# A decoder block in fp32r parts: gate and up of both FFNs as seven block products, in two phases

## The chip, the cores and the metric

The kernel runs on one core of a Trainium2 chip. The metric is the device time of one execution in microseconds. The engines are TensorE (PE in the profile; its weight loads are PEld), VectorE (DVE), ScalarE (ACT), GpSimd (POOL) and SyncE (SP), which only issues transfers here.

## What is computed

One layer for 1,024 tokens with 1,024 channels: an FFN, a merge of three mixers (RWKV-7, sparse attention, attention onto memory tokens), a second FFN and a last norm.

```python
def _rmsnorm(x, g):
    xf = x.astype(jnp.float32)
    y = xf * lax.rsqrt(jnp.mean(xf * xf, axis=-1, keepdims=True) + NORM_EPS)
    return (y * g.astype(jnp.float32)).astype(x.dtype)

def _swiglu(h, w_gate, w_up, w_down):          # w_gate, w_up: 1024 x 2816, w_down: 2816 x 1024
    return (jax.nn.silu(h @ w_gate) * (h @ w_up)) @ w_down

x = x + 0.5 * _swiglu(_rmsnorm(x, ffn1_norm[l]), ffn1_w_gate[l], ffn1_w_up[l], ffn1_w_down[l])
h = _rmsnorm(x, mix_norm[l])
...                                            # the three mixers, merged
x = x + merged @ w_out[l]
x = x + 0.5 * _swiglu(_rmsnorm(x, ffn2_norm[l]), ffn2_w_gate[l], ffn2_w_up[l], ffn2_w_down[l])
return _rmsnorm(x, final_norm)
```

## The kernel before

Everything is held transposed: channels on the partitions in eight tiles (index k or d), tokens in two halves of 512 columns. A number is split into two parts of the type fp32r, a high one (ScalarE, line 71) and the rest (VectorE, line 74); `mm3` (lines 87 to 89) makes a product of three matmuls: high by high, high by rest, rest by high. `wload` (line 76) loads a piece of a weight, 128 x 512, through SyncE's queue into one of two raw buffers and splits it into one of three buffers of each part.

`ffn` (line 174) goes through the 22 column tiles f of gate and up in four chunks of 6, 6, 5 and 5. For each f, gate and up (gu) and both halves, 8 x 3 matmuls with 512 columns add up in one PSUM bank (`pgu`). A weight piece serves both halves. After the four sums of an f the activation is made (lines 250 to 262): tanh on ScalarE, two or three products on VectorE, and the split into `ah` and `al`, which stay on the chip. After the f of a chunk, `down` (line 190) multiplies them with the matching part of the down weights for each of eight output tiles d and adds the sum into x (line 204). In the last chunk the halves run one after the other, and `after` (in `finish`, line 1294) follows each finished tile of x with its square.

The sum of squares of a norm is taken on TensorE: each of the eight squares is split, and two matmuls with a matrix of ones add it up in the bank `nps` (lines 104 to 109). In the first half of the first FFN the squares are not split, and a matrix of ones in fp32 is used (line 106). `rstd` (line 111) makes 1 / rms of the sum. In the first FFN h is x times the norm's gain alone (line 1349), and 1 / rms is multiplied in behind the matmuls (lines 256 and 261). In the second one h is normalized first (line 133).

The steps of the memory tokens (`Mem.tokens`, line 1139) are written into the third chunk of the first FFN. The kernel is written as one order of instructions with tiles and pools; a scheduler places the instructions of each engine and sets all waits. An engine then runs its own queue in order.

Of the kernel before, what the change touches and what calls it, by code (L numbers as in the profile page):

```python
# [16 lines left out]
S = 1024  # L17
# [3 lines left out]
CHUNKS = (6, 6, 5, 5)  # L21
# [5 lines left out]
class Builder:  # L27
    def __init__(self, ctx, tc, A):
        self.ctx, self.tc, self.nc, self.A = ctx, tc, tc.nc, A
        self.cst = ctx.enter_context(tc.tile_pool(name="cst", bufs=1))  # L30
        self.wp = ctx.enter_context(tc.tile_pool(name="wp", bufs=1))
        self.hp = ctx.enter_context(tc.tile_pool(name="hp", bufs=1))
        self.bg = []
        self.consts()

    def tick(self, n=1):
        """a step of what was put off."""
        for _ in range(n):
            while self.bg:
                try:  # L40
                    next(self.bg[0])
                    break
                except StopIteration:
                    self.bg.pop(0)
# [13 lines left out]

    def load_consts(self):
# [16 lines left out]
    def wload(self, src, n, eng_lo="dve", eng_hi="act", pool=None):  # L76
        raw = self.wp.tile([128, n], FT, name="wraw", tag="wraw", bufs=2)
        self.nc.sync.dma_start(raw, src)
        p, bufs = (pool, 2) if pool else (self.wp, 3)
        hi = p.tile([128, n], FR, name="whi", tag="whi", bufs=bufs)  # L80
        lo = p.tile([128, n], FR, name="wlo", tag="wlo", bufs=bufs)
# [3 lines left out]
    def mm3(self, ps, w, x, start, stop):  # L85
        mm = self.nc.tensor.matmul
        mm(ps, w[0], x[0], start=start, stop=False)  # L87
        mm(ps, w[0], x[1], start=False, stop=False)  # L88
        mm(ps, w[1], x[0], start=False, stop=stop)  # L89

    def square(self, pool, x, whole=False, eng_lo="dve"):
        n = x.shape[-1]
        if whole:
            sq = pool.tile([128, n], FT, name="sq", tag="sqh", bufs=3)
            self.nc.scalar.activation(sq, x, AF.Square)
            return [sq]
        sq = pool.tile([128, n], FT, name="sq", tag="sq", bufs=2)
        self.nc.scalar.activation(sq, x, AF.Square)
        hi = pool.tile([128, n], FR, name="sqh", tag="sqh", bufs=3)
        lo = pool.tile([128, n], FR, name="sql", tag="sql", bufs=3)  # L100
        self.split(hi, lo, sq, eng_lo=eng_lo)
        return hi, lo

    def add_square(self, ps, sq, first, last):
        if len(sq) == 1:
            self.nc.tensor.matmul(ps, self.onef, sq[0], start=first, stop=last)
            return
        self.nc.tensor.matmul(ps, self.ones, sq[0], start=first, stop=False)  # L108
        self.nc.tensor.matmul(ps, self.ones, sq[1], start=False, stop=last)  # L109

    def rstd(self, pool, ps, tag="rst", bufs=2):
        nc = self.nc
        n = ps.shape[-1]
        ms, r, u = [pool.tile([128, HALF], FT, name=t, tag=t, bufs=b)[:, 0:n] for t, b in (("ms", 1), (tag, bufs), ("nu", 1))]
# [4 lines left out]
    def rsqrt(self, r, a, u, src, scale, bias):  # L119
        """a ** -0.5, where a = src * scale + bias."""  # L120
# [6 lines left out]
    def scaled(self, pool, x, r, gcol, c, dst):  # L127
        """columns c of the normalized x in two parts, dst(k) says where to."""
        nc = self.nc
        for k in range(KT):  # L130
            t = pool.tile([128, c.stop - c.start], FT, name="hn", tag="sq", bufs=2)
            xk = x(k) if callable(x) else x[k][:, c]
            nc.vector.scalar_tensor_tensor(t, xk, self.vec[:, gcol + k:gcol + k + 1], r,
                                           op0=OP.mult, op1=OP.mult)
            self.split(*dst(k), t)
            yield

    def htile(self, h, half, k):
        """the two parts of h[half][k], which take the place of those of the h before."""
# [5 lines left out]
    def proj(self, pieces, h, evict, halves=(0, 1)):  # L145
        """columns of h @ w for all tokens, transposed; evict(half, PSUM)."""
# [9 lines left out]
    def proj_steps(self, pieces, h, evict, n, halves=(0, 1)):  # L156
        """proj in steps of n parts of the sums."""
# [16 lines left out]
    def ffn(self, x, h, wgu, wd, after, first=None, own=None, aside=None):  # L174
# [3 lines left out]
        nc, tc = self.nc, self.tc  # L178
        halves = [slice(0, HALF), slice(HALF, S)]
        with ExitStack() as st:  # L180
            hp = st.enter_context(tc.tile_pool(name="ffh", bufs=1, reuse_waits="tile"))
            own = own or hp
            ps = st.enter_context(tc.tile_pool(name="ffp", bufs=1, space=PSUM, reuse_waits="tile"))

            def mms(p, w, half):
                for k in range(KT):
                    wc = slice((k % 4) * 128, (k % 4) * 128 + 128)
                    self.mm3(p, [a[:, wc] for a in w[k // 4]], h[half][k], k == 0, k == KT - 1)

            def down(d, f0, nch, act, hs):  # L190
                w = []
                base = f0 * 128
                for q0 in range(0, nch, 3):
                    q1 = min(q0 + 3, nch)
                    w.append((q0, self.wload(wd[d, :, base + q0 * 128:base + q1 * 128], (q1 - q0) * 128)))
                for half in hs:
                    c = halves[half]
                    p = ps.tile([128, HALF], FT, name="pd", tag="dn", bufs=3)
                    for j in range(nch):
                        q0, ww = w[j // 3]  # L200
                        wc = slice((j - q0) * 128, (j - q0) * 128 + 128)
                        self.mm3(p, [a[:, wc] for a in ww], (act[j][0][:, c], act[j][1][:, c]),
                                 j == 0, j == nch - 1)
                    nc.vector.scalar_tensor_tensor(x[d][:, c], p, 0.25, x[d][:, c], op0=OP.mult, op1=OP.add)  # L204

            f0 = 0
            for ci, nch in enumerate(CHUNKS):
                act = []
                for f in range(f0, f0 + nch):
                    pg = {}  # L210

                    def one(gu, half, w):
                        pg[gu, half] = ps.tile([128, HALF], FT, name="pgu", tag="gu", bufs=4)
                        mms(pg[gu, half], w, half)

                    if f == 0:
                        ws = [[None] * 2 for _ in range(2)]

                        def load(gu, q):
                            ws[gu][q] = self.wload(wgu[0, gu, q], 512, pool=own if gu else None)  # L220

                        r, steps = None, None
                        if first:
                            r = {}
                            steps = first(load, r)
                        else:
                            for gu in range(2):
                                for q in range(2):
                                    load(gu, q)
                        for half in range(2):  # L230
# [1392 lines left out]
```

## Time and profile before

| | |
|---|---|
| Time, three runs | 3029.24, 3033.96 (median), 3037.49 us |
| Span of the profiled execution | 3027.2 us |
| TensorE busy | 2952.4 us, 98%, 14,332 matmuls |
| VectorE, ScalarE, GpSimd busy | 1617.0, 1165.5, 308.5 us |
| Moved by DMA | 227.28 MB, 75 GB/s on the mean |

The span runs from the first to the last instruction of the profiled execution; the times of the runs hold what lies around it too. A busy time is the sum of the stretches in which an engine worked; records of matmuls overlap, so the mean length of one is more than its share of the span.

### The profile page before, as it was taken

The numbers are of one execution on the slowest core, as the hardware profiler recorded it, in microseconds if no ns is written. First come the engines' busy times: TensorE is split into PE (matmuls) and PEld (weight loads), VectorE is DVE, ScalarE is ACT, GpSimd is POOL, SyncE is SP. The second block draws the span as 40 slices with busy tenths as digits, with TensorE's granted clock in tenths as the row PEclk, the third lists the DMA queues.
The fourth block names the chain that finished last, engine by engine and source line by source line (L and its number), as shares of the span: only waits on it lengthen the run. The fifth ranks groups of instructions, "written<-read, shape, count | busy, mean of one in ns | idle before, by whom it ended". The sixth has DMA issues, their size and how long they took to land. (4 is left out here: it accounts for less than half of the span.)

```text
span 3027.2 us, 39650 instructions
## 1 busy us (share of the span) xinstructions
PE 2952.4 (98%) x14332; PEld 2352.6 (78%) x14332; DVE 1617.0 (53%) x3674; ACT 1165.5 (39%) x2541; POOL 308.5 (10%) x487
## 2 busy tenths in 40 slices
PE   9999999999999999999999989999999999999998
PEld 6888888887887677777767777777777888888886
DVE  6434334447566556766654367889764323333336
ACT  6212112225454345544543356666453212112124
POOL 0000000000112011111110134333200000000000
PEclk9999999999999999999999999999999999999999
DMA  3111111214313222222121742222541111111113
GB/s 132 45 51 49 47 52 43 65 46 140 107 55 97 61 66 69 69 68 70 59 65 58 196 127 85 76 60 82 173 137 52 45 53 49 45 54 41 55 43 117
DMA packets 170913, 227.28 MB, mean 75 GB/s; under 512 B 42675, under 2 KB 86587, under 8 KB 170716
## 3 DMA queue, kind: packets, MB, share of 16 engines
q1 hardware_dynamic: 154256, 196.13, 21.8%
q10 hardware_dynamic: 16460, 28.61, 3.3%
q8 instruction: 113, 1.85, 0.3%
q14 instruction: 84, 0.69, 0.1%
HBM read 185.76 MB, written 38.91 MB: 74 GB/s over the span
## 5 line engine op out<-in xcount | busy, mean ns | idle before, releaser
L71 ACT ACTIVATE whi<-wraw 128x512 fp32r<-128x512 f32 (+2 forms) x540 | 318.0, 590 | 803.5 <-PE pd L88 307.2
L87 PE MATMUL pgu<-h,whi 128*128 128x512 f32 x1408 | 551.3, 392 | 2.6 <-ACT h L71 2.3
L88 PE MATMUL pgu<-h,whi 128*128 128x512 f32 x1408 | 550.6, 391 | 0.0
L89 PE MATMUL pgu<-h,wlo 128*128 128x512 f32 x1408 | 549.3, 390 | 0.0
L74 DVE TENSOR_TENSOR wlo<-wraw,whi 128x512 fp32r<-128x512 f32 (+2 forms) x532 | 350.1, 659 | 317.2 <-ACT whi L71 315.8
L87 PE MATMUL mm<-h,whi 128*128 128x512 f32 x800 | 330.2, 413 | 0.2 <-ACT gbt L1389 0.2
L89 PE MATMUL mm<-h,wlo 128*128 128x512 f32 x800 | 321.3, 403 | 7.2 <-DVE wlo L74 7.2
L88 PE MATMUL mm<-h,whi 128*128 128x512 f32 x800 | 318.5, 398 | 0.0
L87 PEld LDWEIGHTS pgu<-h,whi 128*128 128x128 f32 x1408 | 265.1, 188 | 61.1 <-ACT h L71 5.3
L88 PEld LDWEIGHTS pgu<-h,whi 128*128 128x128 f32 x1408 | 265.1, 188 | 57.1 <-DVE h L74 1.9
L89 PEld LDWEIGHTS pgu<-h,wlo 128*128 128x128 f32 x1408 | 265.1, 188 | 55.4 <-issue 0.4
L87 PE MATMUL pd<-ah,whi 128*128 128x512 f32 x704 | 275.1, 391 | 0.0
L88 PE MATMUL pd<-al,whi 128*128 128x512 f32 x704 | 274.8, 390 | 0.0
L89 PE MATMUL pd<-ah,wlo 128*128 128x512 f32 x704 | 274.8, 390 | 0.0
L89 PEld LDWEIGHTS mm<-h,wlo 128*128 128x128 f32 x800 | 151.9, 190 | 39.8 <-DVE wlo L74 8.6
L204 DVE SCALAR_TENSOR_TENSOR x<-pd,x 128x512 f32<-128x512 f32 x128 | 88.5, 691 | 174.5 <-PE pd L89 174.4
L87 PEld LDWEIGHTS mm<-h,whi 128*128 128x128 f32 x800 | 151.9, 190 | 36.1 <-issue 5.3
L259 DVE TENSOR_TENSOR sg<-sg,pgu 128x512 f32<-128x512 f32 x88 | 60.5, 688 | 215.5 <-PE pgu L89 215.4
L88 PEld LDWEIGHTS mm<-h,whi 128*128 128x128 f32 x800 | 152.1, 190 | 28.6 <-issue 3.0
L71 ACT ACTIVATE ah<-sg 128x512 fp32r<-128x512 f32 x88 | 55.6, 632 | 263.6 <-DVE sg L261 141.5
L89 PEld LDWEIGHTS pd<-ah,wlo 128*128 128x128 f32 x704 | 132.2, 188 | 28.4 <-DVE wlo L74 0.3
L87 PEld LDWEIGHTS pd<-ah,whi 128*128 128x128 f32 x704 | 132.2, 188 | 28.2 <-ACT whi L71 0.3
(367 smaller groups left out, 4979.5 us busy)
## 6 DMA issues: line engine op xcount, KB each, us to landing
wraw<-in_wgu SPq DMA_DIRECT2D x176, 256.0 KB, 2.6
wraw<-in_wd SPq DMA_DIRECT2D x112, 192.0 KB, 2.3
wraw<-in_win SPq DMA_DIRECT2D x52, 256.0 KB, 2.6
wraw<-in_wgb SPq DMA_DIRECT2D x48, 256.0 KB, 2.7
gd<-gbt SPq DMA_DIRECT2D x48, 256.0 KB, 2.0
gbt<-gd ACTq DMA_DIRECT2D x40, 256.0 KB, 2.7
wraw<-in_wbr SPq DMA_DIRECT2D x32, 256.0 KB, 3.0
wraw<-in_wo SPq DMA_DIRECT2D x32, 256.0 KB, 2.7
```

Of the source, the lines that this page charges most:

```text
L71: nc.scalar.activation(hi, src, AF.Copy)
L74: (nc.vector if eng_lo == "dve" else nc.gpsimd).tensor_sub(lo, src, hi.bitcast(FT))
L87: mm(ps, w[0], x[0], start=start, stop=False)
L88: mm(ps, w[0], x[1], start=False, stop=False)
L89: mm(ps, w[1], x[0], start=False, stop=stop)
L204: nc.vector.scalar_tensor_tensor(x[d][:, c], p, 0.25, x[d][:, c], op0=OP.mult, op1=OP.add)
L259: nc.vector.tensor_mul(sg, sg, pg[1, half])
```

## The change

- The sums of squares: the squares are added up elementwise (`add_square`, by GpSimd, the last one by VectorE), and `rstd` splits the sum and takes it through one pair of ones-matmuls.
- The FFN runs in two phases. In the first, `Gates` makes the activations of all 22 f and stores each (256 KB) to DRAM. In the second, `tail` loads them again, splits them and runs the down products in chunks of 5, 8, 5 and 4, with tiles of its own or in the place of h.
- f = 0 and 1 run as before, half by half (`plain`). The other 20 are taken in ten pairs. For a pair and for gate or up, the product is one of 2 x 2 blocks: two column tiles by two halves of the channels, against two halves of the channels by two halves of the tokens. It is made of seven products of blocks (`run`) in place of eight, after Winograd's form of Strassen's scheme. A product has 4 k x 3 matmuls. Four sums of blocks of h are made once (`sums`), four sums of weights for each pair and gu (`blocks`, on GpSimd), and each of the seven weight blocks is split for itself. The results are put together from three PSUM banks with copies on ScalarE and additions on VectorE. The parts of a weight are split three products ahead (`AHEAD`).
- Both operands of the block products need the full norm: in the first FFN the second half of h is normalized before its matmuls, and the first half of x is loaded and normalized once more after `plain`.
- x is not held on the chip in the first phase: in the first FFN it is loaded again for `tail`, in the second one x and the normalized first half go through DRAM. A ring of ten buffers holds pieces of x and passing values.
- The weights have a pool of their own in each stage, with eight raw buffers and four of each part in the FFNs.

The diff, cut to its core:

```diff
+CHUNKS = (("p", 5), ("h", 8), ("p", 5), ("t", 4))
+RING = 10
+AHEAD = 3
...
+    def add_square(self, pool, acc, x, eng):
...
+        sq = pool.tile([128, HALF], FT, name="sq", tag="sq", bufs=2)[:, 0:n]
         self.nc.scalar.activation(sq, x, AF.Square)
+        eng.tensor_add(acc, acc, sq)
+        return acc
+
+    def rstd(self, pool, pspool, acc, parts=1):
...
+        self.split(hi, lo, acc)
+        ps = pspool.tile([128, HALF], FT, name="nps", tag="nps", bufs=1)[:, 0:n]
+        for e in range(parts):
+            for p, a in enumerate((hi, lo)):
+                nc.tensor.matmul(ps, self.ones, a[:, e * n:e * n + n], start=e + p == 0, stop=e + p == parts)
...
+    def tail(self, x, wd, ad, xload, after, aside=None, st=None):
...
+        def loads(kind, f0, n):
+            got = []
+            for j in range(n):
+                t = parts(kind, j)
+                for half in range(2):
+                    raw = self.wraw(ad[f0 + j][half], HALF)
+                    self.split(*t[half], raw)
+                got.append(t)
+                yield got
...
+class Gates:
...
+    def finish(self, f, half, gu, c, r=None):
...
+            nc.scalar.activation(th, c, AF.Tanh, scale=0.5)
+            sg = self.sg[f, half] = self.p.tile([128, HALF], FT, name="sg", tag="sg", bufs=5)
+            nc.vector.scalar_tensor_tensor(sg, th, 1.0, c, op0=OP.add, op1=OP.mult)
+            return
+        sg = self.sg.pop((f, half))
+        nc.vector.tensor_mul(sg, sg, c)
+        if r is not None:
+            nc.vector.tensor_mul(sg, sg, r)
+        nc.sync.dma_start(self.ad[f][half], sg)
...
+    def sums(self, h, k, raw):
...
+        add.tensor_sub(a11, a12, a11)
+        add.tensor_sub(a12, a22, a12)
+        nc.vector.tensor_sub(a22, a22, a11)
+        add.tensor_sub(a21, a21, a22)
+        for n, a in ((1, a11), (2, a22), (3, a12)):
+            t = [self.tp.tile([128, HALF], FR, name=f"t{p}{n}{k}") for p in range(2)]
+            B.split(*t, a)
...
+    def blocks(self, m):
...
+        a = {(i, q): B.wraw(self.wgu[2 * pair + i, gu, q], 512) for i in range(2) for q in range(2)}
+        yield B.wparts(a[0, 0])
+        yield B.wparts(a[0, 1])
+        s1, s2 = self.temp(), self.temp()
+        nc.gpsimd.tensor_add(s1, a[1, 0], a[1, 1])
+        nc.gpsimd.tensor_sub(s2, s1, a[0, 0])
+        yield B.wparts(s2)
+        yield B.wparts(s1)
+        nc.gpsimd.tensor_sub(a[1, 0], a[0, 0], a[1, 0])
+        yield B.wparts(a[1, 0])
+        yield B.wparts(a[1, 1])
+        nc.gpsimd.tensor_sub(a[0, 1], a[0, 1], s2)
+        yield B.wparts(a[0, 1])
...
+    def product(self, ps, w, x, start, stop):
+        for k in range(4):
+            wc = slice(k * 128, k * 128 + 128)
+            self.B.mm3(ps, [a[:, wc] for a in w], x[k], start and k == 0, stop and k == 3, skip_group_check=True)
...
+        for m in ms:
+            ops += [(m, "P1")] + [(last, "P4")] * (last is not None) + [(m, "P2")] + [(last, "P3")] * (last is not None)
+            ops += [(m, n) for n in ("P6", "P5", "P7")]
+            last = m
+        ops += [(last, "P4"), (last, "P3")]
...
+        for i, (m, name) in enumerate(ops):
+            while len(got) < min(len(ops), i + 1 + AHEAD):
+                pull()
...
+            self.product(ps, w, moving[name], name in ("P1", "P2", "P5"), name in ("P2", "P4", "P3"))
+            if name == "P1":
+                st["s1"] = copy(ps)
+            elif name == "P2":
+                self.finish(2 * pair, 0, gu, add(st["s1"], ps))
+            elif name == "P6":
+                st["u2"] = copy(ps)
+            elif name == "P7":
+                self.finish(2 * pair + 1, 1, gu, add(copy(ps), st["z"]))
+            elif name == "P4":
+                self.finish(2 * pair + 1, 0, gu, ps)
+            elif name == "P3":
+                self.finish(2 * pair, 1, gu, add(st["u2"], ps))
...
+            F.plain(0, hu[0], lambda: r[0], early, more)
+            B.load_consts()
+            xt, acc = [], None
+            for k in range(KT):
+                xt.append(loadx(1, k))
+                acc = B.add_square(np_, acc, xt[k], nc.gpsimd)
+            r[1] = B.rstd(np_, nps, acc)
+            for k in range(KT):
+                B.normed(xt[k], xt[k], r[1], g1 + k)
+                B.split(*B.htile(h, 1, k), xt[k])
+            F.plain(1, h[1])
```

## Rows read from the trace of the kernel before

**Rows 1.** The page's first part: busy us (share of the span) xinstructions.
```profile
PE 2952.4 (98%) x14332; PEld 2352.6 (78%) x14332; DVE 1617.0 (53%) x3674; ACT 1165.5 (39%) x2541; POOL 308.5 (10%) x487
```

**Rows 2.** A stretch of the second FFN: busy us (xinstructions) by engine, clock, DMA.
```profile
core 0: us, PE busy (x) PEld busy (x) DVE busy (x) ACT busy (x) POOL busy (x), PEclk, DMA share, GB/s
2400.00:2600.00 200.00, 200.00 (x884) 165.59 (x884) 61.05 (x94) 38.76 (x66) 0.00 (x0) 1.00 0.17 48
```

**Rows 3.** Groups of matmuls by form: xcount | busy us, mean ns | idle before.
```profile
L87 PE MATMUL pgu<-h,whi 128*128 128x512 f32 x1408 | 551.3, 392 | 2.6 <-ACT h L71 2.3 <-DVE x L1509 0.3
...
L109 PE MATMUL nps<-sql,ones 128*128 128x512 f32 x56 | 22.9, 409 | 1.3 <-DVE sql L74 1.2
...
L106 PE MATMUL nps<-sq,onef 128*128 128x512 f32 x16 | 8.7, 660 | 4.7 <-DVE hn L1349 4.7
```

**Rows 4.** The same view, splits, evictions and elementwise work of the other engines.
```profile
L74 DVE TENSOR_TENSOR wlo<-wraw,whi 128x512 fp32r<-128x512 f32 x372 | 267.7, 721 | 232.0 <-ACT whi L71 231.5
...
L71 ACT ACTIVATE whi<-wraw 128x512 fp32r<-128x512 f32 x380 | 239.3, 631 | 466.5 <-PE pgu L88 232.8 <-PE mm L88 102.3 <-PE pd L88 45.2
...
L259 DVE TENSOR_TENSOR sg<-sg,pgu 128x512 f32<-128x512 f32 x88 | 60.5, 688 | 215.5 <-PE pgu L89 215.4
...
L257 ACT ACTIVATE sg<-gr 128x512 f32<-128x512 f32 x44 | 27.8, 632 | 86.7 <-DVE gr L256 86.6
...
L257 ACT ACTIVATE sg<-pgu 128x512 f32<-128x512 f32 x44 | 25.9, 589 | 88.9 <-PE pgu L89 88.9
...
L1442 POOL TENSOR_TENSOR gbt<-gbt 128x512 f32<-128x512 f32 x16 | 21.4, 1338 | 61.2 <-DVE gbt L1440 28.7 <-issue 27.2 <-DVE mx L1002 3.0
```

**Rows 5.** Timeline of VectorE and GpSimd near 2190 us: start us, us, what.
```profile
2190.39 0.69 DVE L74 TENSOR_TENSOR sql<-sq,sqh 128x512 fp32r<-128x512 f32 x1
...
2191.16 1.62 DVE L74 TENSOR_TENSOR wlo<-wraw,whi 128x512 fp32r<-128x512 f32 x1
...
2190.56 1.68 POOL L1457 TENSOR_TENSOR gl<-gl,pl 128x512 f32<-128x512 f32 x1 [7.75 <-DVE gl L1456]
```

**Rows 6.** A stretch of the middle, columns as in rows 2.
```profile
2100.00:2130.00 30.00, 28.90 (x167) 23.30 (x168) 28.85 (x92) 20.46 (x59) 10.96 (x14) 1.00 0.42 123
```

**Rows 7.** Stretches, of instructions on the tile pgu alone.
```profile
0.00:20.00 20.00, 12.69 (x35) 7.34 (x36) 0.00 (x0) 0.00 (x0) 1.00 0.88 303
20.00:30.00 10.00, 7.13 (x30) 5.37 (x29) 0.00 (x0) 0.00 (x0) 1.00 0.24 79
30.00:40.00 10.00, 7.51 (x32) 5.67 (x32) 1.37 (x2) 0.00 (x0) 1.00 0.18 53
40.00:60.00 20.00, 18.32 (x81) 14.86 (x80) 3.34 (x5) 0.00 (x0) 1.00 0.29 91
...
2270.00:2300.00 30.00, 17.03 (x66) 13.47 (x67) 1.37 (x2) 0.60 (x1) 0.94 0.22 62
2300.00:2320.00 20.00, 20.00 (x89) 16.36 (x88) 2.74 (x4) 1.77 (x3) 1.00 0.13 40
```

**Rows 8.** Timeline of SyncE's queue at the start of the kernel.
```profile
40.45 11.92 SPq L1153 DMA_DIRECT2D mx<-in_memT  x7
```

**Rows 9.** Timeline of VectorE at the starts of the two FFNs.
```profile
17.00 1.29 DVE L74 TENSOR_TENSOR h<-hn,h 128x512 fp32r<-128x512 f32 x2 [0.48 <-ACT h L71]
...
2279.82 0.69 DVE L1509 SCALAR_TENSOR_TENSOR x<-wo,x 128x512 f32<-128x512 f32 x1 [0.64 <-PE wo L89]
...
2292.86 1.41 DVE L133 SCALAR_TENSOR_TENSOR hn<-x,vec,rst 128x512 f32<-128x512 f32 x2
```

**Rows 10.** The chain that ended last, in order of time: start us, us, what.
```profile
3012.38 0.64 ACT sqh L71
...
3017.94 0.75 DVE x L1536
```

**Rows 11.** Timeline of TensorE around 2235 us.
```profile
2235.16 0.50 PE L87 MATMUL wo<-h,whi 128*128 128x512 f32 x1 [1.29 <-ACT h L71]
...
2236.84 0.63 PE L109 MATMUL nps<-sql,ones 128*128 128x512 f32 x1
...
2239.82 0.43 PE L87 MATMUL wo<-h,whi 128*128 128x512 f32 x1
```

More of the change, by code (lines that the diff above doesn't have):

```diff
@@ L57, in consts, with open_w @@
         nc.vector.memset(self.eps, 1e-6)
+    def open_w(self, st, raw=2, parts=3):
+        self.wp = st.enter_context(self.tc.tile_pool(name="wp", bufs=1, reuse_waits="tile"))
+        self.wbufs = raw, parts
     def load_consts(self):
@@ L91, in square @@
-    def square(self, pool, x, whole=False, eng_lo="dve"):
+        mm(ps, w[0], x[0], start=start, stop=False, **kw)
+        mm(ps, w[0], x[1], start=False, stop=False, **kw)
+        mm(ps, w[1], x[0], start=False, stop=stop, **kw)
+    def add_square(self, pool, acc, x, eng):
         n = x.shape[-1]
[L93 to L97, printed above, removed]
-        self.nc.scalar.activation(sq, x, AF.Square)
[L99 to L111, printed above, removed]
-        nc = self.nc
-        n = ps.shape[-1]
-        ms, r, u = [pool.tile([128, HALF], FT, name=t, tag=t, bufs=b)[:, 0:n] for t, b in (("ms", 1), (tag, bufs), ("nu", 1))]
+        if acc is None:
+            acc = pool.tile([128, HALF], FT, name="acc", tag="acc", bufs=2)[:, 0:n]
+            self.nc.scalar.activation(acc, x, AF.Square)
+            return acc
@@ L186, in mms @@
                 for k in range(KT):
                     wc = slice((k % 4) * 128, (k % 4) * 128 + 128)
[L188 to L204, printed above, removed]
@@ new lines, in plain @@
+                    B.mm3(ps, [a[:, wc] for a in w[k // 4]], h[k], k == 0, k == KT - 1)
+                if step:
+                    step()
+                self.finish(f, half, gu, ps, r())
+    def sums(self, h, k, raw):
+        B, nc = self.B, self.nc
+        a11, a12, a21, a22 = raw
+        add = nc.gpsimd
+        out = []
+        add.tensor_sub(a11, a12, a11)
[5 more added lines that the diff above has]
+            B.split(*t, a)
+            out.append(t)
+        t = [B.hp.tile([128, HALF], FR, name=f"t{p}4{k}", tag=f"h{p}1{k}") for p in range(2)]
+        B.split(*t, a21)
+        out.append(t)
+        return out
@@ L1292, in body, with finish @@
     halves = [slice(0, HALF), slice(HALF, S)]
-    def finish(x, np_, nps, end, store=None, whole=False):
+    def finish(x, np_, nps, end, store=None):
         st = {}
         def after(half, d):
-            c = halves[half]
-            if d == 0:
-                st[half] = [nps.tile([128, HALF], FT, name="nps", tag="nps", bufs=1), None]
             if store:
                 store(half, d)
-            ps, last = st[half]
-            if last:
-                B.add_square(ps, last, d == 1, False)
-            st[half][1] = B.square(np_, x[d][:, c], whole)
+            xd = x(half, d) if callable(x) else x[d][:, halves[half]]
+            st[half] = B.add_square(np_, st.get(half), xd, nc.vector if d == KT - 1 else nc.gpsimd)
             if d == KT - 1:
@@ L1365, in body @@
-    h = [], []
-    B.ffn(x, hf, A["wgu1"], A["wd1"],
-          finish(x, np_, nps, into(x, np_, VO["mix_norm"], h),
-                 lambda half, d: nc.sync.dma_start(x1d[d][:, halves[half]], x[d][:, halves[half]])), first,
-          mt, M.tokens(mt, np_, nps, VO["mem_norm"]))
+    ad = [[drp.tile([128, HALF], FT, name=f"ad{f}{i}") for i in range(2)] for f in range(22)]
+    x2d = [drp.tile([128, S], FT, name=f"x2d{k}") for k in range(KT)]
+    xnd = [drp.tile([128, HALF], FT, name=f"xnd{k}") for k in range(KT)]
```

428 lines of the change are left out of this document (245 added, 183 removed).

## The prediction

> **What bounds the kernel now.** I read the page's first part first: TensorE is busy for 98% of the span, VectorE for 53%, ScalarE for 39%, GpSimd for little [rows 1]. A busy share says nothing of pace, so next the stretches. In the middle of the second FFN 884 matmuls start in 200.0 us, with no idle time [rows 2]: one 128x512 matmul costs 0.2262 us of TensorE's time. (Its own row says 392 ns [rows 3]; matmuls overlap, so I cost by the pitch.) VectorE works for 61 of those 200 us. In both FFNs what counts is the number of matmuls; time disappears only where one is dropped, and everything else is hidden until it starves TensorE.
>
> **1. Gate and up: minus 108.6 us.** Before, a column tile f costs 2 weights x 2 halves x 8 k x 3 = 96 matmuls, 4,224 in both FFNs, which are the 3 x 1,408 of [rows 3]. After, f = 0 and 1 stay as they are (192 per FFN). Each of the ten other pairs and each of gate and up takes seven products of 4 k x 3 = 12, so 84 instead of 96: 20 sets x 84 = 1,680 instead of 1,920. Dropped: 240 per FFN, 480 x 0.2262 = 108.6 us. The down products stay at 1,056 per FFN.
>
> **2. Squares: minus 20.4 us.** Before, every norm half sums eight squares on TensorE with two ones-matmuls each: 112 of 512 columns (56 on line 108, as many on 109), 16 of 256 for the memory tokens, and in the first half eight fp32 ones in 16 records [rows 3]. After, a half has two. Outside the first FFN's start 84 of 512 and 12 of 256 go: 84 x 0.2262 + 12 x 0.113 (half the pitch, an estimate) = 20.4 us. The squares are now added by GpSimd, at 1.34 us each [rows 4], off the path.
>
> **3. What each set adds beside TensorE: nothing taken, up to 20 us.** A set lasts 84 x 0.2262 = 19.0 us. In it VectorE splits seven weights (0.72 us, [rows 4]) and does seven evictions and sums (0.69), 9.9 us; ScalarE seven splits (0.63), three PSUM copies (0.59) and at most four tanh (0.63), 8.7 us; GpSimd four adds of 1.34, 5.4 us. VectorE and GpSimd take turns where both read SBUF: a GpSimd add began at 2190.56 under a VectorE operation that ended at 2191.08 and took 1.68 us, and the weight split of 2191.16 then took 1.62 instead of 0.69 [rows 5]. Even fully in turn they need 15.3 of 19.0 us. The weights are split three products ahead, 3 x 2.71 = 8.1 us, and at 2100 to 2130 us VectorE at 28.85 and GpSimd at 10.96 of 30 us leave TensorE busy for 28.9 [rows 6]. So I take zero, and half a microsecond per set (40 sets, 20 us) as the bound. The stores to DRAM wait on SyncE's queue for their product, with weight loads behind them; eight raw buffers are two sets, 38 us, of cover. The Trainium skill speaks against the GpSimd adds ("GPSIMD Engine Reference", 4.1 Engine selection: elementwise two-input work belongs on VectorE, GpSimd is about 2x slower). The rows agree (1.34 against 0.69), but on VectorE the four would make 12.7 of 19.0 us, under the same bound.
>
> **4. The start of the first FFN: plus 22.8 us (10 to 34).** Before, the first 35+30+32+81 = 178 gate and up matmuls have started by 60 us [rows 7], the 192nd by 60 + 14 x 0.2262 = 63.2, squares included. After, the question is when the first seven-product set starts, behind the same 192. Instructions don't stay in written order: the memory tokens, written into the third chunk, are loaded at 40 us [rows 8], so what is ready moves up, and VectorE's and GpSimd's work is the limit.
> First half: VectorE finishes the eighth h tile at 17.7 us now, the first of the two from 17.00 [rows 9]; with seven GpSimd adds (9.4 us) in between, some 21; the 48 matmuls on f=0 end near 22, those on f=1 10.9 later, at 33. Second half: before, h went in unscaled, without waiting for the norm. Now it waits for seven more adds (to about 32) and the norm chain of 5.6 us (3012.38 to 3017.94 in [rows 10]): first tile near 39.5, TensorE idle for 6. From 38 VectorE then owes, before the first set: 8 tiles x (1.41 + 1.29) / 2 [rows 9] = 10.8; ten weight splits 6.9; four evictions 2.8; the reloaded first half, as much again, 10.8; three quarters of the sums (3 x 5 x 0.67) 10.0; together 41.3, of which two reloaded tiles (2.7) fit into the wait. GpSimd owes 9 x 1.34 = 12.1. Side by side the set starts at 77, in turn at 89. Nearer to in turn, by rows 5: 86. Against 63.2 that is 22.8 us. If VectorE uses its idle time better, 10; if nothing overlaps, 34.
>
> **5. The start of the second FFN: plus 1 us (minus 4 to plus 6).** Before, its matmuls begin after 2279.82 [rows 9]; 66 + 89 have started by 2320 [rows 7], the 192nd by 2328.4, 5 us behind the pace. After, 96 matmuls on the first half (21.7 us) cover the second half's norm, so the 192 end near 2324 and the first two products, which need no sums, near 2329.5. The third needs the sums: VectorE owes 44 us from 2280 on (16 + 3 weight splits 13.1, evictions 5.5, norm 3.5, tiles 10.8, 16 operations of sums 11.0), GpSimd 16.1: done between 2324 and 2340. Half of the 10.5 us is 5; less the 4.4 won, plus 1.
>
> **6. Smaller terms: plus 11 us.** Switch to the down phase, twice: the last activations are stored, and the first chunk's tiles are split into space that the last set still holds; most of it is free two products (5.4 us) earlier, so 1.5 each, 3 (0 to 12; at worst ten splits of 0.65 in the open). In the last set the fourth product waits for the copy of the seventh: 0.8 each, 1.6. The end and the mixing norm get one more addition of 0.69 in the chain: 1.4. Each wait also drops TensorE's clock: after 1.3 us of waiting at 2233.87, the matmuls from 2236.84 to 2239.82 start 0.43 us apart, the pace of 1.2 GHz, which cost 1.6 us [rows 11]. Three such stretches: 5, in which changed pools at the borders of the middle are held too (0 to 12).
>
> **Sum.** -108.6 - 20.4 + 22.8 + 1 + 3 + 1.6 + 1.4 + 5 = -94.2. The profiled execution's span is 3027.2, its sum 2933.0; the median of the runs shown is 3033.96, 6.8 above it, which I keep: 2939.8 us.
>
> **The rivals.** (a) Late sets: a set loses 1 us to the turns of VectorE and GpSimd or to ScalarE waiting for an add with a PSUM copy behind it: 40 x 1 = 40, 2980 us. For it: the stretched rows of [rows 5]. Against: 15.3 of 19.0 us.
> (b) Slower: the lookahead fails. A weight is split only when the product before it is evicted, since VectorE and ScalarE run their queues in order and the evictions stand in them. Then 0.63 + 0.69 lie open at each of 280 products: 370 us, 3310 us. It decides from 94 / 280 = 0.34 us per product. Against it: three products of 2.71 us and four buffers of each part; before, the same queues keep TensorE without idle time with three.
> (c) The written order holds. Then the sums (some 40 and 29 us), the second half's preparation (18), 14 group borders of 2 us and two switches of 7 are all open, about 129 us, which eats the 129.0 of steps 1 and 2 and leaves about 10 for the squares of the start: near 3025, no change to speak of. Against it: [rows 8].
> (d) A dropped matmul does not give back a whole pitch. A record lasts 392 ns at a pitch of 226, so 166 ns of it lie under its neighbours [rows 2, 3]; if only as much came back, step 1 would be 480 x 0.166 = 79.7 and the time 2969. Against: 884 in 200.0 us leave nothing between them. The Trainium skill ("TensorE: Matmul & The Clock Gate", section Back-to-back issue gap) gives 131 ns per 512-column matmul in a sustained stream, by which step 1 would be 62.9 us and the time 2986; the rows of this trace do not agree with it, and they decide.
>
> **How the numbers follow.** Forecast 0.70; (a) 0.12; (b) 0.08; (c) 0.07; (d) 0.03. A measurement of this kernel can tell about 0.3%, 9 us. Faster: 0.70 + 0.12 + 0.03 and 0.02 of (c), 0.87; within 0.3%: 0.04; slower: (b) and the worst of (c), 0.09. Range: low, steps 4 to 6 at their good ends (-12.8, -5, and -3 and -5 in step 6), 2914, and 6 less, should the squares of the first start, which step 4 holds, be worth more than it allows: 2908; high, steps 3 to 6 at their bad ends (+20, +11, +5, +9, +7), 2992, which holds (a) and (d) too, 0.85 in all less what lies at its ends.
>
> **What would show it.** Right: 3,744 gate and up matmuls at 0.226 us pitch and no idle TensorE in the stretches of sets; idle or thin stretches in the first 90 us alone. Wrong: waits of TensorE for weight parts inside the sets (a, b); source order in the first 100 us (c); a pitch other than 0.226 (d). What would upset the forecast most is a starved start far over 34 us, or GpSimd adds much longer than 1.34.

## The result, and the profile after

The changed kernel takes 3011.7 us (median; 3008.7 to 3016.3), beside 3031.6 us of the kernel before on the same chip: ratio 0.9937, 95% interval 0.9918 to 0.9956. It is faster, by 20 us instead of the 94 forecast, and lies above the range. The profiled execution, the longest of its four, has a span of 3014.5 us, 12.7 less than that of before, which was among the shorter of its own; the account below goes by these two spans.

What was forecast for the sets of seven products is there. A stretch of the second FFN and the groups of matmuls, to be read against [rows 2] and [rows 3]:

```profile
2400.00:2600.00 200.00, 200.00 (x884) 165.61 (x883) 101.77 (x147) 74.04 (x127) 60.84 (x44) 1.00 0.26 81
```

```profile
L97 PE MATMUL pgu<-t,whi 128*128 128x512 f32 x640 | 253.7, 396 | 7.7 <-ACT t L77 4.5 <-ACT rg L370 2.7 <-ACT whi L77 0.5
...
L97 PE MATMUL pgu<-h,whi 128*128 128x512 f32 x608 | 241.7, 398 | 15.0 <-ACT h L77 13.8 <-DVE rg L1655 0.9 <-ACT whi L77 0.3
```

3 x (640 + 608) = 3,744 gate and up matmuls, at the pitch of before (884 in 200.0 us), although VectorE now works for 102 us of the 200 and GpSimd for 61. The page's first part shows where the gain went: TensorE has fallen from 98% [rows 1] to 94% busy.

```profile
PE 2842.3 (94%) x13728; PEld 2252.2 (75%) x13728; DVE 1772.1 (59%) x3825; ACT 1289.0 (43%) x2752; POOL 640.7 (21%) x724
```

The waits of TensorE (us in all, times, longest) name the places:

```profile
PE pd L97 <- ACT whi L77: 38.5, 2, 19.5
PE nps L122 <- ACT sqh L77: 15.9, 3, 10.2
PE pgu L97 <- ACT h L77: 13.8, 5, 5.9
PE pgu L98 <- DVE h L80: 11.9, 10, 2.9
PE wo L97 <- ACT whi L77: 8.2, 1, 8.2
```

38.5 us lie ahead of the two down phases, 8.2 ahead of wo, the rest of these rows at the two starts. There, the stretches of instructions on the tile pgu that answer to [rows 7]:

```profile
0.00:20.00 20.00, 10.48 (x24) 6.68 (x25) 0.00 (x0) 0.00 (x0) 1.00 0.80 289
20.00:30.00 10.00, 8.30 (x35) 6.24 (x34) 0.00 (x0) 0.00 (x0) 1.00 0.35 105
30.00:40.00 10.00, 9.03 (x40) 7.13 (x38) 2.65 (x4) 0.00 (x0) 1.00 0.65 197
40.00:60.00 20.00, 3.68 (x9) 2.49 (x10) 0.00 (x0) 0.00 (x0) 0.57 0.28 100
60.00:80.00 20.00, 20.00 (x90) 16.48 (x89) 2.04 (x3) 1.18 (x2) 1.00 0.34 105
80.00:100.00 20.00, 10.38 (x21) 4.83 (x19) 0.68 (x1) 0.00 (x0) 0.59 0.28 91
100.00:120.00 20.00, 14.64 (x35) 9.02 (x35) 0.68 (x1) 1.16 (x2) 0.56 0.09 25
120.00:140.00 20.00, 20.00 (x89) 16.56 (x89) 2.74 (x4) 2.33 (x4) 1.00 0.27 83
...
2320.00:2340.00 20.00, 17.20 (x75) 13.61 (x73) 2.04 (x3) 0.58 (x1) 0.99 0.39 118
2340.00:2360.00 20.00, 12.21 (x26) 7.34 (x27) 0.68 (x1) 1.16 (x2) 0.59 0.20 64
```

TensorE stands open in two holes in the first FFN (under the second half's norm, 40 to 60 us, at a granted clock of 0.57; under the sums of h, 80 to 120, at 0.59 and 0.56) and in one in the second. SyncE's queue ahead of and in these holes, first for x's second half, then for the first half's reloads, and VectorE's first use of the second half's scale:

```profile
21.61 10.84 SPq L84 DMA_DIRECT2D wraw<-in_wgu  x6
32.50 1.37 SPq L1448 DMA_DIRECT2D rg<-in_xT  x3
...
42.95 27.83 SPq L84 DMA_DIRECT2D wraw<-in_wgu  x7
...
73.58 3.85 SPq L1448 DMA_DIRECT2D rg<-in_xT  x2
...
85.93 12.44 SPq L1448 DMA_DIRECT2D rg<-in_xT  x6
```

```profile
54.81 2.08 DVE L147 SCALAR_TENSOR_TENSOR rg<-rg,vec,rst 128x512 f32<-128x512 f32 x3
```

Last, SyncE's queue at the first switch to the down phase, and the first down matmul (in brackets the idle time ahead of it, and what ended it):

```profile
485.75 6.11 SPq L288 DMA_DIRECT2D ad<-sg  x3
492.14 0.92 SPq L84 DMA_DIRECT2D wraw<-ad  x2
493.16 5.09 SPq L1496 DMA_DIRECT2D x<-in_xT  x8
498.45 1.67 SPq L84 DMA_DIRECT2D wraw<-in_wd  x2
```

```profile
509.09 0.80 PE L97 MATMUL pd<-a,whi 128*128 128x512 f32 x1 [19.03 <-ACT whi L77]
```

Eight loads of x, 4 MB, go out ahead of the first two loads of down weights.

**Where the 81 us of the miss lie.** The spans put it at 12.7 won instead of 94.2. By the starts of the last `x<-pd` (750.89, then 755.01; 3010.99, then 2995.52) and the last sum with wo (2279.82 [rows 9], then 2284.43):

| stretch, us | before | after | difference | forecast |
|---|---|---|---|---|
| first FFN | 750.9 | 755.0 | +4.1 | -36.9 |
| middle and wo | 1528.9 | 1529.4 | +0.5 | -5.6 |
| second FFN | 731.2 | 711.1 | -20.1 | -57.3 |
| end | 16.2 | 19.0 | +2.8 | +0.7 |

(The forecast's 5 us for clock and pools belong to no single row.) Each switch costs its wait plus ten matmuls behind it at 0.427 us, the pace of the 1.2 GHz level (granted clock 0.50 from 509 to 513 us): 19.0 + 2.0 and 19.5 + 2.0. With the dropped matmuls at full price (-62.0 and -60.6) and 0.8 for the last set, 44.3 us are left for the first start and 18.2 for the second. Counted in the stretches, the first is 195 matmuls behind at 140 us (343 against 178 + 360), 44.1 us. The two ways agree with the squares at full price; at none, 36.6 us would be left.

### The profile page after: what moved, and what is told of

It reads as the page before. It is cut to its first block, busy times and chain, and to the rows that moved or that the text cites. A ratio compares the mean times of both kernels' runs of the same rounds, so it can differ in the third digit from the quotient of the medians.

```text
span 3014.5 us, 39899 instructions
## 1 busy us (share of the span) xinstructions
PE 2842.3 (94%) x13728; PEld 2252.2 (75%) x13728; DVE 1772.1 (59%) x3825; ACT 1289.0 (43%) x2752; POOL 640.7 (21%) x724
## 5 line engine op out<-in xcount | busy, mean ns | idle before, releaser
L77 ACT ACTIVATE whi<-wraw 128x512 fp32r<-128x512 f32 (+1 forms) x564 | 343.8, 612 | 828.1 <-PE pgu L98 266.8
L80 DVE TENSOR_TENSOR wlo<-wraw,whi 128x512 fp32r<-128x512 f32 (+1 forms) x556 | 396.0, 714 | 411.9 <-ACT whi L77 355.2
L97 PE MATMUL pd<-a,whi 128*128 128x512 f32 x704 | 276.1, 392 | 38.5 <-ACT whi L77 38.5
L99 PE MATMUL pd<-a,wlo 128*128 128x512 f32 x704 | 275.4, 391 | 0.6 <-DVE wlo L80 0.6
L98 PE MATMUL pd<-a,whi 128*128 128x512 f32 x704 | 275.5, 391 | 0.0
L97 PE MATMUL pgu<-t,whi 128*128 128x512 f32 x640 | 253.7, 396 | 7.7 <-ACT t L77 4.5
L99 PE MATMUL pgu<-t,wlo 128*128 128x512 f32 x640 | 252.4, 394 | 5.6 <-DVE wlo L80 5.6
L97 PE MATMUL pgu<-h,whi 128*128 128x512 f32 x608 | 241.7, 398 | 15.0 <-ACT h L77 13.8
L98 PE MATMUL pgu<-t,whi 128*128 128x512 f32 x640 | 252.8, 395 | 3.0 <-DVE t L80 3.0
L98 PE MATMUL pgu<-h,whi 128*128 128x512 f32 x608 | 242.4, 399 | 11.9 <-DVE h L80 11.9
L99 PE MATMUL pgu<-h,wlo 128*128 128x512 f32 x608 | 239.8, 395 | 1.2 <-DVE wlo L80 1.2
L97 PEld LDWEIGHTS pd<-a,whi 128*128 128x128 f32 x704 | 133.2, 189 | 66.8 <-ACT whi L77 39.4
L99 PEld LDWEIGHTS pd<-a,wlo 128*128 128x128 f32 x704 | 133.0, 189 | 29.3 <-DVE wlo L80 1.5
L98 PEld LDWEIGHTS pd<-a,whi 128*128 128x128 f32 x704 | 133.3, 189 | 27.8
```

The costliest lines, as they stand in the source:

```text
L77: nc.scalar.activation(hi, src, AF.Copy)
L80: (nc.vector if eng_lo == "dve" else nc.gpsimd).tensor_sub(lo, src, hi.bitcast(FT))
L97: mm(ps, w[0], x[0], start=start, stop=False, **kw)
L98: mm(ps, w[0], x[1], start=False, stop=False, **kw)
L99: mm(ps, w[1], x[0], start=False, stop=stop, **kw)
```

## Experiments

All ratios are to the kernel before, with the 95% interval; the changed kernel stands at 0.9937. Edits are cut to their core, and the words behind a # are added.

**Squares alone (e1).** The kernel before with the new sums of squares outside the first start:

```diff
-            if last:
-                B.add_square(ps, last, d == 1, False)
-            st[half][1] = B.square(np_, x[d][:, c], whole)
+            st[half][1] = B.acc_square(np_, last, x[d][:, c], nc.vector if d == KT - 1 else nc.gpsimd)
```

> The kernel before with the squares' part of the change alone (outside the first FFN's start): squares of a norm half are added up by GpSimd and one pair of ones-matmuls sums them; FFNs as before. My sum (step 2): 84 matmuls of 512 and 12 of 256 columns fewer, minus 20.4 us against the kernel before (ratio 0.9933), less 1.4 for the one more addition in the chain at the end: about minus 19. Rival: the squares were matmuls that filled waits of the wo and down stretches, and the chain at each norm gets longer by GpSimd's additions: minus 8 or less (ratio over 0.9974).

Measured: 0.9977 (0.9967 to 0.9988), 7 us. The last down stretch of before, of this kernel and of the changed one (busy us of TensorE, its weight loads, VectorE, ScalarE, GpSimd; clock; DMA):

```profile
715.00:752.00 37.00, 36.21 (x163) 29.16 (x161) 28.78 (x50) 23.93 (x44) 2.59 (x2) 1.00 0.49 155
```

```profile
715.00:752.00 37.00, 31.52 (x129) 22.25 (x129) 30.07 (x44) 17.73 (x34) 10.68 (x8) 1.00 0.43 136
```

```profile
715.00:752.00 37.00, 37.00 (x166) 30.63 (x165) 27.80 (x39) 19.21 (x33) 17.00 (x13) 1.00 0.37 123
```

Without the squares TensorE starts 34 matmuls fewer in the same 37 us and waits instead for VectorE's weight rests (4.4 us in six waits). VectorE is held up too: five of its operations there started under one of GpSimd's additions and took 0.9 to 1.1 us longer than their like. Here is a rest of 256 columns under the addition that began at 742.59 and took 1.72 us, then one of the kernel before:

```profile
743.09 1.50 DVE L74 TENSOR_TENSOR wlo<-wraw,whi 128x256 fp32r<-128x256 f32 x1
```

```profile
743.13 0.42 DVE L74 TENSOR_TENSOR wlo<-wraw,whi 128x256 fp32r<-128x256 f32 x1
```

How much of the lost gain is this and how much the rests themselves is open: no run has the additions on VectorE. By the dates of the table above the two FFNs of e1 are 0.4 and 0.1 us shorter, where step 2 priced 7.7 and 6.3; what is won lies between them. In the changed kernel that stretch is full: its last group has four column tiles instead of five and more weight buffers (which of the two, was not tried). So the step's size holds together with the other parts, not by itself.

**A product dropped (e2).**

```diff
-            self.product(ps, w, moving[name], ...)
+            if name != "P6":
+                self.product(ps, w, moving[name], ...)
```

> The changed kernel without the twelve matmuls of product P6 in each of the 40 sets, so it leaves out part of the sums; the weights of P6 are still loaded, added and split, and all evictions stay. 480 matmuls fewer, as many as the change itself took out. If a dropped matmul gives back the whole pitch and nothing but TensorE bounds the sets, it is 480 x 0.2262 = 108.6 us faster than the changed kernel (about 2903, ratio to the kernel before 0.958). Rival (d): 0.166 us each, 79.7 us (about 2932, 0.967). Rival (a): the sets are already bound by VectorE and GpSimd in turn, then under 60 us (over 2952, 0.974).

Measured: 0.9585 (0.9564 to 0.9606), 2906.9 us; 0.0352 x 3032 = 107 us for 480 matmuls, 0.222 each. Step 1 stands, rivals (a) and (d) fall. A set without P6 still fills TensorE, with VectorE at 125 of 200 us:

```profile
200.00:400.00 200.00, 200.00 (x884) 165.60 (x883) 124.67 (x171) 85.57 (x147) 68.57 (x51) 1.00 0.31 96
```

By the Trainium skill ("TensorE: Matmul & The Clock Gate", Back-to-back issue gap), 131 ns per matmul in a sustained stream, an estimate for 480 is 62.9 us; the measured 107 us do not agree, and they decide.

**x behind the down weights (e3), and weights first (e8).**

```diff
-        for d in range(KT):
-            xload(d)
+            if then:            # in down(), behind the weight loads of d, first group only
+                then(d)         # then = xload
```

> The changed kernel, but in both down phases the load of x's tile d is issued behind the down weights of d (in the first group) instead of all eight ahead of the first weights. Theory 'order of SyncE's queue': the 4 MB of x, 12 to 13 us of transfers, stand ahead of the first down weights while TensorE waits 19 us; each switch gets 8 to 13 us shorter, the kernel 16 to 26 us faster than the changed kernel (2986 to 2996, ratio to the kernel before 0.985 to 0.988). Rival 'work': the first group's ten rest-splits on VectorE and the activations coming back from DRAM set the switch; under 5 us in all (0.992 or more).

Measured: 0.9869 (0.9849 to 0.9888), 2992.4 us. The weights go out at 494.74 instead of 498.45, with one tile of x behind them, not eight ahead:

```profile
494.74 0.94 SPq L84 DMA_DIRECT2D wraw<-in_wd  x2
495.79 0.36 SPq L1496 DMA_DIRECT2D x<-in_xT  x1
```

```profile
499.73 0.80 PE L97 MATMUL pd<-a,whi 128*128 128x512 f32 x1 [8.28 <-ACT whi L77]
```

The wait is 8.28 us instead of 19.03. e8 also puts the first weights ahead of the last two activation tiles:

```diff
-        for a[0] in gens[0]:
-            pass
+        for i, a[0] in enumerate(gens[0]):
+            if i == 2:
+                pre[0, 0] = weights(0, 0, CHUNKS[0][1])
```

> As the run with x's loads behind the down weights, and the first two weight loads of the down phase are issued ahead of the last three of the first group's five activation tiles. There 8.28 us were left at the switch, of which the weights landing behind the last activations are some. Theory 'order of SyncE's queue': 3 to 6 us less at each switch, 2981 to 2987 (ratio to the kernel before 0.983 to 0.985). Rival: VectorE's ten rests of the activations (6.1 us, all behind the last eviction) set what is left; under 2 us each (0.9855 or more).

Measured: 0.9821 (0.9799 to 0.9843), 2980.2 us.

```profile
478.61 2.98 SPq L85 DMA_DIRECT2D wraw<-in_wd  x2
```

```profile
491.69 0.61 PE L98 MATMUL pd<-a,whi 128*128 128x512 f32 x2
```

The first down matmul starts at 491.69, 17.4 us earlier than in the changed kernel, and VectorE's ten rests cost a wait of 1.66 us. The order of the loads was 0.0116 of the time, 35 of the 42.5 us at the switches.

**The second half of x early (e4).**

```diff
+            xt = [loadx(1, k) for k in range(KT)]     # ahead of F.plain(0, ...)
```

> The changed kernel, but in the first FFN the loads of x's second half are issued before the weight loads of f = 1 instead of behind them. Theory 'order of SyncE's queue': second half's squares start near 25 instead of 37 us, its scale is there some 12 us earlier, and the first sets start 8 to 14 us earlier (2998 to 3004, ratio to the kernel before 0.989 to 0.991). Rival 'work': VectorE and GpSimd taking turns over the tiles, weight splits and sums set when the sets start, whenever x comes; under 4 us (0.9925 or more).

Measured: 0.9932 (0.9913 to 0.9952), nothing. The scale came 6.2 us earlier (48.63 us; 54.81 in the changed kernel), the first reloads of the first half 2.2 us earlier (71.36; 73.58), behind weight loads as before, and the first subtraction of the sums 2 us earlier (78.86; 80.90). By itself the earlier scale does not count; which of the two theories is right showed only in e13.

**Weight buffers in one place (e5).**

```diff
+        if i % all_ < own:
+            return self.wp0.tile([128, n], dt, name=t, tag=t, bufs=own)     # open all along
         return self.wp.tile([128, n], dt, name=t, tag=t, bufs=all_ - own)
```

> The changed kernel, but a part of the weight buffers (two raw, three of each split part) stays in one place for the whole kernel, as in the kernel before, and only the rest is opened for the FFNs; so wo's weights can be loaded while the middle still runs. Theory 'new pool': at 2169.75 us TensorE has waited 8.19 us for wo's first split weight, whose load was issued at 2160.16 (kernel before: 2143.46) because the new buffers lie where the middle still worked. Minus 6 to 10 us (3002 to 3006, ratio to the kernel before 0.990 to 0.992). Rival: the middle's own end or the loads of x1 set that time; under 3 us (0.993 or more).

Measured: 0.9912 (0.9895 to 0.9929), 3005.8 us; the gain of 8 us is about as large as what the two intervals leave open. The trace agrees: the first loads of wo go out 13 us earlier, and the wait ahead of wo's matmuls is 4.1 us, in one piece, instead of 8.2.

```profile
2147.13 6.82 SPq L93 DMA_DIRECT2D wraw<-in_wo  x3
```

**Sums on VectorE (e6).**

```diff
-        add = nc.gpsimd
+        add = nc.vector
```

> The changed kernel, but all four subtractions of the sums of h per k are VectorE's (three were GpSimd's). Rival 'turns': near 100 us one k takes 8.9 us (GpSimd's first subtraction at 98.01, the next k's at 106.90 in the run with the early x), as a chain that hops between GpSimd (1.65, 1.60, 1.66 us) and VectorE; without the hops and the stretched operations each start gains 6 or more, 12 or more in all (ratio to the kernel before under 0.990). Theory 'work': VectorE has two scalings of 0.74, two rests of 0.68, four subtractions of 0.69 and four rests of 0.68 per k, 8.3 us, so the gain is 0.6 us per k, 5 in all (0.991 to 0.9935).

Measured: 0.9890 (0.9871 to 0.9910), 2999.7 us, at the rival's end. One k of the changed kernel on GpSimd, from its first subtraction to the next one's, and the same on VectorE:

```profile
99.96 1.65 POOL L311 TENSOR_TENSOR rg<-rg 128x512 f32<-128x512 f32 x1 [2.50 <-DVE h L80]
101.69 1.61 POOL L312 TENSOR_TENSOR rg<-rg 128x512 f32<-128x512 f32 x1
104.70 1.66 POOL L314 TENSOR_TENSOR rg<-rg 128x512 f32<-128x512 f32 x1 [1.41 <-DVE h L80]
108.87 1.65 POOL L311 TENSOR_TENSOR rg<-rg 128x512 f32<-128x512 f32 x1 [2.50 <-DVE h L80]
```

```profile
98.62 0.68 DVE L311 TENSOR_TENSOR rg<-rg 128x512 f32<-128x512 f32 x1
...
106.08 0.69 DVE L311 TENSOR_TENSOR rg<-rg 128x512 f32<-128x512 f32 x1
```

8.9 us against 7.5: the idle time in brackets and the stretched 1.65 us go. The rule of the Trainium skill that the prediction weighed ("GPSIMD Engine Reference", 4.1 Engine selection: two-input elementwise work on VectorE, GpSimd about twice as slow) holds here, where the subtractions stand in the path (1.61 to 1.66 against 0.68 us).

**No sums (e9).** `sums()` returns parts of h.

> The changed kernel without the sums of h (no subtractions and no splits of T1 to T4 in either FFN): the products take parts of h instead, so it leaves out part of the computation; matmuls, weights, reloads and scaling of the first half stay. It prices the sums at the two starts. From the trace of the changed kernel: from 80 to 120 us TensorE starts 56 matmuls of the 178 that two full stretches hold (27.6 us lost), from 2320 to 2360 101 of 179 (17.6 us). Theory 'sums': they are most of what lies open there; minus 30 to 40 us (2972 to 2982, ratio to the kernel before 0.980 to 0.984). Rival: the second half's norm and the reloaded tiles set the first sets as much; minus 15 or less (0.9885 or more).

Measured: 0.9756 (0.9742 to 0.9771), 2959.5 us, 55 us less, more than expected, since a second thing went: x was loaded at the start (first and last issue 30.0 and 47.9 us; the room left by the tiles of the sums is the likely reason), and the switches shrank from 38.5 to 15.2 us.

```profile
L1481 SPq DMA_DIRECT2D x<-in_xT x8: 328/328/425, 30.0 to 47.9; - x8
```

```profile
PE pd L97 <- ACT whi L77: 15.2, 2, 8.2
```

That is e3's finding by another way. By stretches: first FFN 27.4 less, 10.8 of it at the switch, so the sums are 16.6, less what x's early loads cost that start (from 40 to 60 us e9 starts no gate or up matmul, the changed kernel 9); second 30.9 less, 12.5 of it, so 18.4. The second start is the sums alone (18.2 by the table); in the first, up to 28 us are something else.

**One more plain pair, with and without the early x (e7, e13).**

```diff
-        for f in range(2):            # plain()
+        for f in range(4):
...
-        ms = [(pair, gu) for pair in range(1, 11) for gu in range(2)]
+        ms = [(pair, gu) for pair in range(2, 11) for gu in range(2)]
```

> The changed kernel with one more pair of column tiles (f = 2 and 3) done plainly in each FFN ahead of the sums, so nine pairs by seven products instead of ten; and the rests of the fourth sum are made behind the others, since they go where the second half's h lies. 24 matmuls more per FFN, 5.4 us each. Theory 'no cover': TensorE stands open under the second half's norm (49 to 60 us) and under the sums (80 to 117 us); 96 matmuls more (21.7 us) ahead of each cover some of both; with the price taken off, 10 to 30 us faster than the changed kernel (ratio to the kernel before 0.983 to 0.990). Rival: the 16 further weight splits per FFN (11.5 us of VectorE) push the sums back by as much as is covered; no gain or up to 11 us slower (0.993 or more).

> The changed kernel with one more plain pair in each FFN and, besides, x's second half loaded ahead of the weights of f = 1 to 3. In the run with the plain pair alone those loads moved from 32.50 to 54.55 us and TensorE was busy for 4.1 of the 20 us from 60 to 80. Theory 'order of loads': the second half's scale comes near 49 us, under the plain products, that hole closes, 12 to 16 us faster than that run (ratio to the kernel before 0.991 to 0.993). Rival 'work': VectorE's further splits and evictions push the second half's tiles behind 70 us all the same; under 5 us (0.995 or more).

Measured: 0.9968 (0.9957 to 0.9980) and 0.9929 (0.9914 to 0.9943). In e7 x's second half went out at 54.55 us, behind the further weight loads, its scale was used from 76.97, and the hole only moved; with the early x it was used from 66.75 and the hole nearly closed. TensorE from 60 to 80 us in e7, then in e13:

```profile
60.00:80.00 20.00, 4.13 (x10) 1.95 (x9) 9.56 (x13) 9.42 (x14) 9.52 (x7) 0.58 0.31 110
```

```profile
60.00:80.00 20.00, 14.26 (x55) 10.89 (x54) 17.23 (x27) 10.19 (x15) 0.00 (x0) 0.83 0.20 57
```

So the order of loads made that hole, 12 us between the two runs. Against the changed kernel e13 is level within the noise: what the cover won went into the price of the pair (10.9 us). From 80 to 120 us VectorE was busy for 20.4 of 40, the sums ran from 111 to 151, and the first half's reloads had gone out behind weight loads again:

```profile
104.51 2.92 SPq L84 DMA_DIRECT2D wraw<-in_wgu  x2
107.49 4.04 SPq L1452 DMA_DIRECT2D rg<-in_xT  x2
```

**Together (e10, e11, e12, e14).** e10 is e8, e5 and e6 in one kernel; e11 adds the early x, e12 the early x and twelve ring buffers, e14 the early x and the plain pair.

> The changed kernel with four edits together: x's loads behind the down weights, the first down weights ahead of the last activations, the weight buffers in part in one place, the sums on VectorE. If the causes are separate, the gains of the single runs add up: ratio to the kernel before 0.9937 less 0.0116, 0.0025 and 0.0047, 0.975 (0.973 to 0.977; 2950 to 2963 us). Rival: they share one cause (the transfers that land at the start of each stretch), then 0.979 or more.

> As the run with the four edits together, and x's second half loaded ahead of the weights of f = 1. In the changed kernel this gave nothing although the second half's scale came 6 us earlier (48.63 instead of 54.81 us). Theory 'work': VectorE's queue behind it (weight splits, tiles, sums: busy for 19.65 of 20 us from 80 to 100 with the sums on it) decides, so within 2 us of the run without it (0.973 to 0.977). Rival: it was GpSimd's part that took the gain, then 4 to 8 us faster (under 0.9735).

> As the run before it (four edits and the early second half), with twelve buffers instead of ten in the ring from which x's tiles, the reloaded first half and the evictions take theirs. Six reloads of the first half wait for such buffers on SyncE's queue (11 to 12.5 us for six, from 84 to 97). Theory 'ring': with two more the reloads come earlier and the sums start earlier, 3 to 6 us. Rival 'work': VectorE has no idle time there, so within 2 us of the run with ten.

> The same two edits on top of the four combined ones (x behind the down weights, down weights first, weight buffers in one place, sums on VectorE), whose ratio was 0.9765. If the hole at 40 to 60 us closes and the sums have more cover, it outweighs the 10.9 us of 48 more matmuls: 0.970 to 0.975 (2942 to 2957 us). Rival: the cover is eaten by the additional splits on VectorE, and the price stays: 0.977 to 0.980.

Measured: e10 0.9765 (0.9752 to 0.9779), 2960.5 us: the single gains nearly add up (0.975 expected). e11 0.9772 (0.9758 to 0.9787), e12 0.9757 (0.9742 to 0.9772): no difference. e14 0.9789 (0.9770 to 0.9808): 5 us slower than e11, which lacks only the pair. That is less than the intervals tell apart, but no gain.

**Reloads and sums between the plain products (e15, e16).**

```diff
-            F.plain(1, h[1])
...
+            mk = make()                   # one step after each product: loads of k, or sums of k
+            F.plain(1, h[1], then=mk)
```

> The four edits, the early second half and twelve ring buffers (ratio to the kernel before 0.9757), and in both FFNs the reload and the sums of each k are written between the plain products of the second half instead of behind them. Theory 'order': VectorE is busy for 13.4 of the 20 us from 60 to 80, so some 6 us of the sums move up there at each start, 4 to 10 us faster in all (0.9725 to 0.9745). Rival 'work': those 6 us are waits of VectorE for split weights that stay, no gain (0.975 to 0.977).

> As the run beside it, with one more plain pair in each FFN (price 10.9 us), so that there are eight plain products of the second half to write reloads and sums between. Theory 'order': the 20 of 40 us that VectorE idled before 120 us take in most of the sums, TensorE has no hole behind them, 12 to 18 us faster than four edits with the plain pair (0.9789): 0.973 to 0.975. Rival 'work': the hole only moves again, 0.978 or more.

Both also make the rests of the fourth sum last, as e7 does.

Measured: e15 0.9788 (0.9775 to 0.9802), 9 us slower than e12: with only four products to write between, weight rests came behind the sums on VectorE's queue, and TensorE waited 20.1 us for one. e16 0.9716 (0.9697 to 0.9735), 2944.3 us, is 12 us faster than e12 and 22 faster than e14, more than was expected. The reloads go out from 80.29 us and VectorE is busy ahead of 120:

```profile
80.29 0.89 SPq L1469 DMA_DIRECT2D rg<-in_xT  x2
```

```profile
80.00:100.00 20.00, 20.00 (x90) 16.57 (x89) 18.25 (x30) 12.37 (x21) 0.00 (x0) 1.00 0.52 166
100.00:120.00 20.00, 17.46 (x73) 13.09 (x71) 20.00 (x29) 10.67 (x19) 7.92 (x5) 1.00 0.39 127
120.00:140.00 20.00, 13.41 (x48) 10.93 (x49) 12.84 (x20) 6.65 (x11) 6.36 (x5) 0.74 0.20 60
```

## Why the prediction was right in sign and wrong in size

By size the 81 us are 39.5 at the switches, 21.5 at the first start, 17.2 at the second, 6.1 in the middle and 2.1 at the end, less the 5 set aside for clock and pools.

- **Steps 1 and 3** held: 3,744 matmuls, the old pitch, no wait of TensorE in the sets (140 to 480 and 2380 to 2715 us), 0.222 us for a dropped matmul (e2).
- **Step 2** held in the changed kernel, where both last down stretches are full (37.00 of 37 us from 715, 40.00 of 40 from 2950); alone it gives 7 us (e1), and nothing in the FFNs: the weight rests come next there, and GpSimd's additions, which step 2 put off the path, lengthen VectorE's operations. The prediction priced the squares by the pitch without asking what comes next in that stretch.
- **Step 6, the switch**, failed most: 3 us forecast, 42.5 measured. The prediction counted the splits of ten activation tiles and not that x's 4 MB are loaded there too, into room that the sets hold to the end, on the queue of the down weights and ahead of them. e3, e8 and e9 show it: 35 of the 42.5 us go with the order alone. Step 6 also let each wait drop TensorE's clock, from one row. The waits of 19 us did so; the one of 1.66 us in e8 did not (granted clock 1.00 from 491 to 500 us, the matmuls behind it 0.23 us apart).
- **Step 4** failed next: 22.8 forecast, 44 measured, beyond its bound of 34. It took VectorE's and GpSimd's work as the limit and let the second half's scale be there at 38 us. But x's second half waited on SyncE until 32.50, behind weight loads, and the scale was used from 54.81, 17 us late. From there to the end of the sums (116.85) it took 62 us, where the forecast had 48 to the first set (38 to 86): the first half's reloads queued behind weight loads as well (73.58, the last six from 85.93). The rate of the sums was about right (8.9 us per k, between 6.1 side by side and 10.1 in turn by the prediction's own prices). How the 21 us missed divide between the late scale and the late reloads is not shown: the scale alone, 6.2 us earlier, gives nothing (e4). With products to run and each load in its place most of the hole closes (e13, e16).
- **Step 5**: 1 forecast, 18 measured, all of it sums (18.4, e9). The bounds had them done by 2340 at the latest, under and just behind 96 matmuls; the trace has them until 2358 (GpSimd's last subtraction 2354.66). The reloads for them were issued from 2324.48 on, behind weight loads; that these set the date, and not the work on VectorE and GpSimd, was not tried by itself.
- **The middle's border** was in step 6's 5 us for clock and pools: 8.2 us of wait, half of it gone in e5.
- **The rivals**: (a), (b) and (d) did not happen. (c) came nearer to the measured time (3025) than the forecast, with a chance of 0.07, but partly by luck: its 14 group borders of 2 us are not in the trace, and its switches of 7 us cost 21. It is right in that loads keep their place in a queue, wrong in that all work keeps the written order: weight loads moved up ahead of x. The evidence that moved the prediction away from it, the memory tokens loaded at 40 us [rows 8], showed that loads move up; it did not show what they move ahead of.

With the four edits, the early x, twelve ring buffers, the further plain pair and the sums between its products the kernel takes 2944 us. That this is close to the forecast for the change as it was is chance: the edits are not in the forecast. In e16 the first start is still 98 matmuls, 22 us, short of full pace from 60 to 80 and 100 to 140 us (51, 73 and 48 of 90); these were not followed further.

## What to carry to other kernels

Where a phase changes, list the loads on each queue in their order, with the buffer that each waits for: a big transfer that nobody needs yet, ahead of a small one that TensorE waits for, cost as much here (35 us) as the sums of h at the two starts (16.6 and 18.4). Date a preparation that opens a phase by the issue of its last load, then by its chain from engine to engine. Cover without an earlier load won nothing, nor did an earlier load without cover (e7, e4). With the load early, the further products and the reloads written between products each won nothing alone (e14, e15); together they were worth 12 us (e16 against e12).

## What the runs showed of the hardware beside this

GpSimd's 128x512 subtraction takes 1.27 to 1.29 us alone and mostly 1.59 to 1.80 beside VectorE's two-input work; VectorE's rests beside it went from 0.68 to some 1.75. In the sets, with VectorE at 102 and GpSimd at 61 of 200 us, none of this cost TensorE anything; in the chain of the sums it did (e6), and in the last down stretch of e1 it may have. Out of a wait of 19 us TensorE came back at the pace of 1.2 GHz for ten matmuls (509.09 to 513.52, granted clock 0.50), 2 us lost.
